# Delta rule: 16x16 diagonal blocks inverted by substitution on VectorE, chunks prepared ahead through DRAM

## The chip, the cores and the metric

One core of a Trainium2 chip runs the whole program in one launch. The metric is the device time in microseconds (us) of one execution. The kernel before was run three times: median 2832.96 us, from 2828.85 to 2835.94 us. One more execution was profiled.

## The reference, cut to what matters

The program is two transformer blocks over 1024 tokens of width 1024, in float32: a first mixer (retention beside a gated delta rule), a mixture of experts, a second mixer and an MLP. The change touches the gated delta rule alone. Per head and per chunk of tokens it computes

```python
a_mat = where(tri_strict, (k_beta @ k.T) * decay, 0.0)
t_mat = triangular_solve(eye + a_mat, eye, lower=True, unit_diagonal=True)
u = t_mat @ v_beta
w = t_mat @ (k_beta * exp(g))
attn = (q @ k.T) * decay
def step(state, inp):
    v_new = u_n - w_n @ state
    o_n = qg_n @ state + attn_n @ v_new
    state = state * gl_n + kt_n.T @ v_new
    return state, o_n
```

so one unit lower triangular matrix is inverted per head and chunk, and a state of 128x128 per head goes from chunk to chunk.

## The kernel before, in words

Every instruction is recorded first and placed later. The class `Program` takes each call with what it reads and writes (`record`, whose call of the engine is the line 346 that nearly all rows of the profile carry), gives it a price (`price`), and `flush` lists the instructions engine by engine with a list scheduler: an engine takes, of the instructions that are ready by the planned times, the one with the longest remaining path, and `prog.boost` is added to that length. The order is then fixed: on the chip every engine runs its own list in order and waits on semaphores. All loads and stores go through the one queue of SyncE (SP), also in a fixed order. Tiles are slots of two SBUF areas (`sbuf_61` for float32, `sbuf_62` for float32r in the listings of order below); a slot that is used again makes its new writer wait for the old readers. PSUM banks are handed out round robin by tag: `acc` has two, `dn` three, `tp`, `rs` and `rt` one each.

The first mixer (`mixer1`) makes the normed input, projects and convolves the delta rule's q, k and v into the DRAM buffer `qkv_d` (`dn_project`), and then records three things whose instructions the scheduler mixes:

- `dn_chunks` (line 1022), 8 chunks of 128 tokens with 4 heads, at boost 40000. Each 128x512 tile holds the four heads side by side.
- `tok_blocks`, boost 0: five blocks of 512 columns of `w_in` over 8 token tiles, each tile 24 float32r matmuls of 512 columns, evicted by ACT, DVE and POOL and stored to `rq_d`, `rk_d`, `rv_d`, `zg_d`; beside them eight half rows of `w_ada` are multiplied on DVE (`matvec`) and stored to `mod_d`.
- `retention`, 8 chunks, boost 40000; it needs what `tok_blocks` stores.

Then `mix_out` follows, the router, the experts, the second mixer and the MLP.

A chunk of `dn_chunks` loads k, q and v from `qkv_d`; transposes k, takes its norms, scales it (`kh`) and transposes it back (`khT`); makes the decays (`E`, `dN`, `dT`) and multiplies them with the products of `khT` with itself and with q. `dN` is then the strictly lower matrix to be inverted, `dT` the attention. The inverse is built by doubling in seven levels, b = 1, 2, 4, ... 64: `Uf` holds the inverse transposed and `Ti` the inverse, both right in blocks of b; a level masks the blocks that it adds out of `dN` (`AM`, on POOL) and runs

```python
mm(pp[:, h, :], AM[:, h, :], Uf[:, h, :], start=True, stop=True)
nc.scalar.activation(P, pp, AF.Copy)
mm(pu[:, h, :], Ti[:, h, :], P[:, h, :], start=True, stop=True)
nc.vector.tensor_tensor(out=Uf, in0=Uf, in1=pu, op=OP.subtract)
if b < 64:
    tr(pt[:, h, :], Uf[:, h, :], self.ident)
    nc.vector.tensor_copy(Ti, pt)
```

for h in 0 to 3, each step waiting for the one before on another engine. Level b = 1 needs only four transposes, two subtractions and a mask. After the levels come the products with the state `S`, the new state `Sn` and the output `o`, which is stored to `mix_d`.

Of the kernel before, what the change touches and what calls it, by code (L numbers as in the profile page):

```python
# [21 lines left out]
T = 1024  # L22
# [490 lines left out]
def shape_constants():  # L513
# [47 lines left out]
class Kern:  # L561
# [459 lines left out]

    def dn_chunks(self, A):
        nc, pd, sc = self.nc, self.pd, self.sc
        mm, tr = nc.tensor.matmul, nc.tensor.transpose
        S = None

        def bc(a, n=128):
            return a[:, :, None].to_broadcast([128, 4, n])

        lv = (1, 2, 4, 8, 16, 32, 64)  # L1030
        m3 = {b: A[f'm{b}'][:, None, :].to_broadcast([128, 4, 128]) for b in lv}
        eye3 = self.ident[:, None, :].to_broadcast([128, 4, 128])
        for n in range(NT):
            self.prog.boost = 40000.
            beta, G = sc['beta'][:, n], sc['G'][:, n]
            lq, lk, lv_ = [self.t(pd, [128, 4, 128], tag='ld' + c, bufs=2 if c == 'q' else 1) for c in 'qkv']
            for dst, i in ((lk, 1), (lq, 0), (lv_, 2)):
                nc.sync.dma_start(dst, self.qkv_d[:, 4 * i:4 * i + 4, n * 128:(n + 1) * 128])
            qT = lambda h: lq[:, h, :]

            ssk = self.t(pd, [128, 8], tag='ssk', bufs=2)
            junk = self.t(pd, [128, 128], tag='djunk', bufs=1)
            pk = self.ps([128, 4, 128], 'tp')
            for h in range(4):
                tr(pk[:, h, :], lk[:, h, :], self.ident)
            for h in range(4):
                nc.scalar.activation(junk, pk[:, h, :], AF.Square, accum_out=ssk[:, h:h + 1])
            rk = self.rstd(pd, ssk[:, 0:4], 4, 1.0, 'rk')
            kh = self.t(pd, [128, 4, 128], tag='kh', bufs=2)
            nc.vector.tensor_tensor(out=kh, in0=pk, in1=bc(rk), op=OP.mult)  # L1050
            pT = self.ps([128, 4, 128], 'tp')
            for h in range(4):
                tr(pT[:, h, :], kh[:, h, :], self.ident)
            khT = self.t(pd, [128, 4, 128], tag='khT', bufs=2)
            nc.scalar.activation(khT, pT, AF.Copy)
# [17 lines left out]
            nc.gpsimd.tensor_tensor(out=dT, in0=E, in1=A['negT'][:, None, :].to_broadcast([128, 4, 128]), op=OP.add)
            nc.scalar.activation(dT, dT, AF.Exp)
            pa = self.ps([128, 4, 128], 'dn')
            for h in range(4):
                mm(pa[:, h, :], khT[:, h, :], khT[:, h, :], start=True, stop=True)
            nc.vector.tensor_tensor(out=dN, in0=pa, in1=dN, op=OP.mult)
            pa = self.ps([128, 4, 128], 'dn')
            for h in range(4):  # L1080
                mm(pa[:, h, :], khT[:, h, :], qT(h), start=True, stop=True)
            nc.vector.tensor_tensor(out=dT, in0=pa, in1=dT, op=OP.mult)

            Uf = self.t(pd, [128, 4, 128], tag='U', bufs=2)
            Ti = self.t(pd, [128, 4, 128], tag='Ti', bufs=2)
            for b in lv:
                AM = self.t(pd, [128, 4, 128], tag='AM', bufs=2)
                (nc.vector if b == 1 else nc.gpsimd).tensor_tensor(out=AM, in0=dN, in1=m3[b], op=OP.mult)
                pp = self.ps([128, 4, 128], 'dn')
                if b == 1:  # L1090
                    for h in range(4):
                        tr(pp[:, h, :], AM[:, h, :], self.ident)
                    nc.vector.tensor_tensor(out=Uf, in0=eye3, in1=pp, op=OP.subtract)
                    nc.gpsimd.tensor_tensor(out=Ti, in0=eye3, in1=AM, op=OP.subtract)
                    continue
                for h in range(4):
                    mm(pp[:, h, :], AM[:, h, :], Uf[:, h, :], start=True, stop=True)
                P = self.t(pd, [128, 4, 128], tag='P', bufs=2)
                nc.scalar.activation(P, pp, AF.Copy)
                pu = self.ps([128, 4, 128], 'dn')  # L1100
                for h in range(4):
                    mm(pu[:, h, :], Ti[:, h, :], P[:, h, :], start=True, stop=True)
                nc.vector.tensor_tensor(out=Uf, in0=Uf, in1=pu, op=OP.subtract)
                if b < 64:
                    pt = self.ps([128, 4, 128], 'dn')
                    for h in range(4):
                        tr(pt[:, h, :], Uf[:, h, :], self.ident)
                    nc.vector.tensor_copy(Ti, pt)
            pv = self.ps([128, 4, 128], 'tp')
            for h in range(4):  # L1110
                tr(pv[:, h, :], lv_[:, h, :], self.ident)
            vb = self.t(pd, [128, 4, 128], tag='vb', bufs=1)
            nc.vector.tensor_tensor(out=vb, in0=pv, in1=bc(beta), op=OP.mult)

            if n:
                pw = self.ps([128, 4, 128], 'dn')
                for h in range(4):
# [4 lines left out]
            pv2 = self.ps([128, 4, 128], 'dn')
            for h in range(4):
                mm(pv2[:, h, :], Uf[:, h, :], vb[:, h, :], start=True, stop=True)
            vn = self.t(pd, [128, 4, 128], tag='vn', bufs=1)
            nc.scalar.activation(vn, pv2, AF.Copy)
            o = self.t(pd, [128, 4, 128], tag='o', bufs=1)
            if n:
                po = self.ps([128, 4, 128], 'dn')
                for h in range(4):  # L1130
                    mm(po[:, h, :], qT(h), S[:, h, :], start=True, stop=True)
                nc.vector.tensor_tensor(out=o, in0=po, in1=bc(sc['eG'][:, n]), op=OP.mult)
            po = self.ps([128, 4, 128], 'dn')
            for h in range(4):
                mm(po[:, h, :], dT[:, h, :], vn[:, h, :], start=True, stop=True)
            if n:
                nc.vector.tensor_tensor(out=o, in0=o, in1=po, op=OP.add)
            else:
                nc.vector.tensor_copy(o, po)
            if n < NT - 1:  # L1140
                ktl = self.t(pd, [128, 4, 128], tag='ktl', bufs=1)
                nc.gpsimd.tensor_tensor(out=ktl, in0=kh, in1=bc(sc['etail'][:, n]), op=OP.mult)
                pS = self.ps([128, 4, 128], 'dn')
                for h in range(4):
                    mm(pS[:, h, :], ktl[:, h, :], vn[:, h, :], start=True, stop=True)
                Sn = self.t(pd, [128, 4, 128], tag='S')
                if n:
                    for h in range(4):
                        nc.vector.scalar_tensor_tensor(Sn[:, h, :], S[:, h, :], sc['elast'][:, n, h:h + 1],
# [1137 lines left out]
```

## Time and profile before

| | us |
|---|---|
| median of 3 runs | 2832.96 |
| profiled execution, its own time | 2830.14 |
| span of the profile | 2828.1 |
| TensorE (PE) busy in the span | 2663.9 (94%) |
| delta rule, token blocks and retention side by side | about 213 to 660 |

The page gives the busy time of each engine, then the span in 40 slices with the busy share of a slice in tenths. A group of instructions is listed with its count, its busy time (overlaps counted once), the mean time of one, and the idle time of its engine just before it with what ended it. A matmul's time runs from its start to its modelled end, so successive ones overlap; the time that one occupies the engine is the busy time of a dense run through its count.

### The profile page before, as it was taken

The numbers are of one execution on the slowest core, as the hardware profiler recorded it, in microseconds if no ns is written. First come the engines' busy times: TensorE is split into PE (matmuls) and PEld (weight loads), VectorE is DVE, ScalarE is ACT, GpSimd is POOL, SyncE is SP. The second block draws the span as 40 slices with busy tenths as digits, with TensorE's granted clock in tenths as the row PEclk, the third lists the DMA queues.
The fourth block names the chain that finished last, engine by engine and source line by source line (L and its number), as shares of the span: only waits on it lengthen the run. The fifth ranks groups of instructions, "written<-read, shape, count | busy, mean of one in ns | idle before, by whom it ended". The sixth has DMA issues, their size and how long they took to land. (4 is left out here: it accounts for less than half of the span.)

```text
span 2828.1 us, 36441 instructions
## 1 busy us (share of the span) xinstructions
PE 2663.9 (94%) x13174; PEld 2048.9 (72%) x13174; DVE 1705.0 (60%) x2575; ACT 1117.4 (40%) x1960; POOL 622.5 (22%) x675
## 2 busy tenths in 40 slices
PE   5999999999978999999986999999999999999998
PEld 4787788997757776454435777777888888888886
DVE  7557676555679888786766335277445454444445
ACT  4333223333136677565545434357422212122122
POOL 2106433432442111322136012144110000000001
PEclk9999999999979999999998999999999999999999
DMA  9443246246348999999978343263211111111111
GB/s 243 91 138 88 93 149 165 80 157 230 143 165 287 344 349 341 352 323 361 341 245 295 121 125 110 72 172 94 94 42 52 38 52 52 45 52 53 45 53 67
DMA packets 305621, 446.82 MB, mean 158 GB/s; under 512 B 61274, under 2 KB 135694, under 8 KB 304414
## 3 DMA queue, kind: packets, MB, share of 16 engines
q1 hardware_dynamic: 298782, 427.68, 46.5%
q0 software_dynamic: 6656, 16.79, 1.7%
q8 instruction: 105, 1.72, 0.2%
q14 instruction: 78, 0.64, 0.1%
HBM read 384.54 MB, written 65.75 MB: 159 GB/s over the span
## 5 line engine op out<-in xcount | busy, mean ns | idle before, releaser
L346 PE MATMUL psum_all<-sbuf 128*128 128x512 f32 (+10 forms) x13174 | 2663.9, 363 | 151.7 <-DVE sbuf L346 99.9
L346 PEld LDWEIGHTS psum_all<-sbuf 128*128 128x128 f32 (+7 forms) x13174 | 2048.9, 176 | 766.3 <-issue 167.3
L346 ACT ACTIVATE sbuf<-sbuf 128x1024 fp32r<-128x1024 f32 (+9 forms) x792 | 707.6, 914 | 781.3 <-PE psum_all L346 536.3
L346 DVE TENSOR_TENSOR sbuf<-sbuf,sbuf 128x1024 fp32r<-128x1024 f32 (+3 forms) x538 | 616.8, 1166 | 277.6 <-ACT sbuf L346 269.0
L346 ACT ACTIVATE sbuf<-psum_all 128x512 f32<-128x512 f32 (+14 forms) x798 | 377.9, 485 | 886.1 <-PE psum_all L346 839.7
L346 POOL TENSOR_TENSOR sbuf<-sbuf 128x512 f32<-128x512 f32 (+7 forms) x325 | 384.3, 1190 | 576.7 <-DVE sbuf L346 474.4
L346 DVE TENSOR_TENSOR sbuf<-sbuf,psum_all 128x512 f32<-128x512 f32 (+4 forms) x359 | 239.1, 673 | 165.2 <-PE psum_all L346 164.6
L346 DVE TENSOR_TENSOR sbuf<-sbuf 128x512 f32<-128x512 f32 (+9 forms) x285 | 205.2, 734 | 203.6 <-ACT sbuf L346 175.5
L346 POOL TENSOR_SCALAR sbuf<-sbuf 128x1 f32<-128x1 f32 (+3 forms) x182 | 75.3, 415 | 994.9 <-ACT sbuf L346 902.7
L346 DVE TENSOR_TENSOR sbuf<-psum_all,sbuf 128x512 fp32r<-128x512 f32 (+13 forms) x306 | 182.3, 607 | 158.0 <-ACT sbuf L346 78.1
L346 DVE SCALAR_TENSOR_TENSOR sbuf<-sbuf 128x512 f32<-128x512 f32 (+5 forms) x247 | 196.3, 801 | 55.6 <-POOL sbuf L346 43.1
L346 DVE TENSOR_SCALAR sbuf<-sbuf 128x32 f32<-128x32 f32 (+7 forms) x220 | 111.2, 518 | 48.1 <-ACT sbuf L346 22.7
L1728 POOL DMA_INDIRECT y_d<-sbuf x35 | 57.4, 1641 | 195.8 <-DVE sbuf L346 194.5
L346 DVE SCALAR_TENSOR_TENSOR sbuf<-psum_all,sbuf 128x128 f32<-128x128 f32 (+9 forms) x109 | 62.0, 585 | 40.0 <-PE psum_all L346 39.5
L1716 POOL DMA_INDIRECT sbuf<-h_d,sbuf x35 | 45.1, 1288 | 186.2 <-PE psum_all L346 153.2
L346 DVE SCALAR_TENSOR_TENSOR sbuf<-sbuf,psum_all 128x128 f32<-128x128 f32 (+1 forms) x100 | 38.2, 409 | 76.7 <-PE psum_all L346 51.8
L346 DVE CUSTOM_DVE_ANT_0 sbuf<-psum_all,sbuf 128x512 f32<-128x512 f32 (+2 forms) x80 | 48.1, 613 | 24.8 <-PE psum_all L346 24.2
L346 DVE COPY sbuf<-psum_all 128x512 f32<-128x512 f32 (+9 forms) x55 | 31.7, 576 | 39.9 <-PE psum_all L346 39.7
L346 POOL MEMSET sbuf<- 64x64 f32 (+10 forms) x54 | 16.8, 313 | 174.4 <-DVE sbuf L346 91.9
L346 POOL TENSOR_TENSOR sbuf<-sbuf,sbuf 128x1024 fp32r<-128x1024 f32 x16 | 40.1, 2510 | 61.7 <-ACT sbuf L346 48.4
L346 ACT ACTIVATE sbuf<-psum_all,sbuf 128x128 f32<-128x128 f32 (+1 forms) x72 | 24.4, 405 | 23.4 <-PE psum_all L346 17.7
L346 ACT ACTIVATION_READ_ACCUMULATOR sbuf<-sbuf 128x1 f32 x152 | 28.9, 190 | 0.0
(18 smaller groups left out, 111.8 us busy)
## 6 DMA issues: line engine op xcount, KB each, us to landing
sbuf<-in_w SPq DMA_DIRECT2D x384, 512.0 KB
sbuf<-in_w_ff SPq DMA_DIRECT2D x64, 512.0 KB
sbuf<-in_w_in SPq DMA_DIRECT2D x56, 512.0 KB
sbuf<-in_w_ada SPq DMA_DIRECT2D x48, 512.0 KB
sbuf<-in_x SPq DMA_DIRECT2D x16, 512.0 KB
sbuf<-in_w_out SPq DMA_DIRECT2D x16, 512.0 KB
sbuf<-y_d SPq DMA_DIRECT2D x8, 1024.0 KB
qkv_d<-sbuf SPq DMA_DIRECT2D x12, 512.0 KB
```

Source lines behind the costliest of these rows:

```text
L346: op = self.new_op(eng, lambda: real(*a, **k), name, reads, writes)
L1716: return self.prog.real.gpsimd.indirect_dma_start(out=xg, out_offset=None, in_=self.h2_d, in_offset=bass.IndirectOffsetOnAxis(ap=tok, axis=0),
L1728: st = self.prog.real.gpsimd.indirect_dma_start(out=self.y_d, out_offset=bass.IndirectOffsetOnAxis(ap=dest, axis=0), in_=y, in_offset=None ...
```

## The change

The seven levels become three, b = 16, 32 and 64. What the first four made, the inverses of the 16x16 diagonal blocks, is made by forward substitution on VectorE instead. Four chunks of four heads have 128 such blocks, so each partition takes one, and 30 small instructions (15 steps of a product and a subtraction over 15 to 64 elements) serve four chunks. To bring a block into one partition, `dN` goes to the DRAM buffer `nb_d` and is read back as 128x16x16 in runs of 64 bytes; the inverses and their transposes go through `xb_d`, and each chunk reads its own as 128x4x32 in runs of 128 bytes and spreads them with the mask `blk` into `Uf` and `Ti`.

`dn_chunks` is cut in three: `dn_pre` (norms, transposes, decays, `dN`, `dT`), `dn_blocks` (the substitution) and `dn_scan` (the levels, the state, the output). As chunks are prepared well before their scans, `kh`, `khT`, `dN` and `dT` of a chunk (128x2048, 1 MB) are stored to `pre_d` and loaded again by the scan into a tile `prw` with one buffer; q is loaded twice.

```diff
-    for b in (1, 2, 4, 8, 16, 32, 64):
+    a.add('blk', i[:, None] // 16 == i[None, :] // 16)
+    for b in (16, 32, 64):
...
+        self.prog.boost = 40000.
+        for n in range(4):
+            self.dn_pre(A, n)
+        self.dn_blocks(0)
+        self.dn_scan(A, 0)
+        self.dn_pre(A, 4)
+        self.dn_pre(A, 5)
+        self.dn_scan(A, 1)
+        self.dn_pre(A, 6)
+        self.dn_pre(A, 7)
+        self.dn_blocks(1)
+        for n in range(2, 8):
+            self.dn_scan(A, n)
...
+        nc.vector.tensor_tensor(out=dN, in0=pa, in1=dN, op=OP.mult)
+
+        nc.sync.dma_start(self.dram_ap(self.nb_d, 4 * 16512 * n, [[128, 128], [16512, 4], [1, 128]]), dN)
...
+        nc.vector.tensor_tensor(out=dT, in0=pa, in1=dT, op=OP.mult)
+        nc.sync.dma_start(self.pre_d[n * 128:(n + 1) * 128], W.rearrange("p a h e -> p (a h e)"))
+
+    def dn_blocks(self, s):
+
+        nc, pd, V = self.nc, self.pd, self.nc.vector
+        N = self.t(pd, [128, 512], tag='P', bufs=2)[:, 0:256].rearrange("p (i j) -> p i j", j=16)
+        nc.sync.dma_start(N, self.dram_ap(self.nb_d, 128 * 2064 * s, [[2064, 128], [128, 16], [1, 16]]))
+        X = self.t(pd, [128, 16, 2, 16], tag='AM', bufs=2)
+        Y = self.t(pd, [128, 512], tag='P', bufs=2)[:, 0:256].rearrange("p (i j) -> p i j", j=16)
+        flat = X.rearrange("p i t j -> p (i t j)")
+        V.memset(flat, 0.0)
+        V.memset(flat[:, 0:512:33], 1.0)
+        for i in range(15):
+            r = [128, 15 - i, i + 1]
+            y, x = Y[:, i + 1:, 0:i + 1], X[:, i + 1:, 0, 0:i + 1]
+            V.tensor_tensor(out=y, in0=N[:, i + 1:, i:i + 1].to_broadcast(r),
+                            in1=X[:, i:i + 1, 0, 0:i + 1].to_broadcast(r), op=OP.mult)
+            V.tensor_tensor(out=x, in0=x, in1=y, op=OP.subtract)
+        V.tensor_copy(X[:, :, 1], X[:, :, 0].rearrange("p i j -> p j i"))
+        nc.sync.dma_start(self.xb_d[128 * s:128 * s + 128], flat)
+
+    def dn_scan(self, A, n):
...
+        lq, lv_ = [self.t(pd, [128, 4, 128], tag='ld' + c, bufs=1) for c in 'qv']
+        C = self.t(pd, [128, 4, 2, 16], tag='bC', bufs=2)
+        W = self.t(pd, [128, 4, 4, 128], tag='prw', bufs=1)
+        nc.sync.dma_start(W.rearrange("p a h e -> p (a h e)"), self.pre_d[n * 128:(n + 1) * 128])
+        nc.sync.dma_start(C.rearrange("p h t j -> p h (t j)"),
+                          self.dram_ap(self.xb_d, 32 * 512 * n, [[32, 128], [4096, 4], [1, 32]]))
...
+        for eng, t, x in ((nc.gpsimd, 1, Uf), (nc.vector, 0, Ti)):
+            eng.tensor_tensor(out=x.rearrange("p h (k j) -> p h k j", j=16), in1=blk,
+                              in0=C[:, :, t:t + 1, :].to_broadcast([128, 4, 8, 16]), op=OP.mult)
+        for b in (16, 32, 64):
...
```

The masks of levels 1 to 8 leave the constant `k_a`, whose load shrinks from 1864 to 1480 columns. The program before has 11765 matmuls and transposes, the changed one 11445.

The instructions of all engines differ up to the router's setup in `mix_out`; from there on they stand in the same order. Three places matter.

On TensorE, early in the first chunk before. A row of 128x128 from `sbuf_61` is a step of the delta rule (four heads), a row of 128x512 from `sbuf_62` is the token blocks:

```order
L346 MATMUL psum_all<-sbuf_61 128x128 x4
L346 MATMUL psum_all<-sbuf_62 128x512 x5
L346 MATMUL psum_all<-sbuf_61 128x128 x4
L346 MATMUL psum_all<-sbuf_62 128x512 x6
L346 MATMUL psum_all<-sbuf_61 128x128 x8
L346 MATMUL psum_all<-sbuf_62 128x512 x5
L346 MATMUL psum_all<-sbuf_61 128x128 x4
L346 MATMUL psum_all<-sbuf_62 128x512 x6
L346 MATMUL psum_all<-sbuf_61 128x128 x8
```

And now, where the four chunks are prepared and the first substitution runs:

```order
L346 MATMUL psum_all<-sbuf_61 128x128 x12
L346 MATMUL psum_all<-sbuf_62 128x512 x17
L346 MATMUL psum_all<-sbuf_61 128x128 x4
L346 MATMUL psum_all<-sbuf_62 128x512 x6
L346 MATMUL psum_all<-sbuf_61 128x128 x4
L346 MATMUL psum_all<-sbuf_62 128x512 x46
L346 MATMUL psum_all<-sbuf_61 1x512
L346 MATMUL psum_all<-sbuf_62 128x512 x59
L346 MATMUL psum_all<-sbuf_61 128x128 x4
L346 MATMUL psum_all<-sbuf_62 128x512 x5
L346 MATMUL psum_all<-sbuf_61 128x128 x4
L346 MATMUL psum_all<-sbuf_62 128x512 x6
```

The pattern of a level, 4, then 5, then 4, then 6, then 8, came straight after the preparation; now 46 and 59 matmuls of the token blocks stand between the preparation and the first level, and the second substitution has 30, 29 and 36 in the same way.

On VectorE, the first substitution (128x15 to 128x2x14 are its products and subtractions; 128x4x64 are the rotary products of the token blocks, 128x1024 a weight split):

```order
L346 TENSOR_TENSOR sbuf_61<-sbuf_61 128x15 x2
L346 TENSOR_TENSOR sbuf_61<-sbuf_61 128x4x64
L346 TENSOR_TENSOR sbuf_61<-sbuf_61 128x14x2 x2
L346 TENSOR_TENSOR sbuf_61<-sbuf_61 128x13x3 x2
L346 TENSOR_TENSOR sbuf_61<-sbuf_61 128x12x4 x2
L346 TENSOR_TENSOR sbuf_61<-sbuf_61 128x11x5 x2
L346 TENSOR_TENSOR sbuf_62<-sbuf_61,sbuf_62 128x1024
L346 TENSOR_TENSOR sbuf_61<-sbuf_61 128x10x6 x2
L346 TENSOR_TENSOR sbuf_61<-sbuf_61 128x9x7 x2
L346 TENSOR_TENSOR sbuf_61<-sbuf_61 128x8x8 x2
```

Where before a chunk's subtractions and copies from PSUM stood between the products of the token blocks, 30 small instructions stand now, once for four chunks; with the two shown, 11 instructions of the token blocks and of `matvec` stand among them: seven of 128x4x64, three of 128x512 and one of 128x1024.

On SP's queue, what a chunk asked for before, between the store of the chunk ahead and its own steps:

```order
L346 DMA mix_d<-sbuf_61 128x512
L346 DMA sbuf_61<-in_w_in 128x2x512 x2
L346 DMA sbuf_61<-in_w_ada 128x2x512
L346 DMA sbuf_61<-qkv_d 128x4x128 x2
L346 DMA sbuf_61<-in_w_ada 128x2x512 x2
```

and now, from the store of the first substitution to the load of the second scan's 1 MB:

```order
L346 DMA xb_d<-sbuf_61 128x512
L346 DMA sbuf_61<-in_w_ada 128x2x512
L346 DMA rk_d<-sbuf_61 128x512
L346 DMA sbuf_61<-in_w_ada 128x2x512
L346 DMA mod_d<-sbuf_61 1x512
L346 DMA sbuf_61<-xb_d 128x4x32 x2
L346 DMA sbuf_61<-in_w_ada 128x2x512
L346 DMA rk_d<-sbuf_61 128x512
L346 DMA sbuf_61<-in_b_ada 1x512
L346 DMA sbuf_61<-xb_d 128x4x32 x2
L346 DMA rk_d<-sbuf_61 128x512 x2
L346 DMA sbuf_61<-pre_d 128x2048
```

The store of the inverses and the loads that wait for it stand in line with the stores of the token blocks (`rk_d`) and the loads of `w_ada`.

## Rows read from the trace of the kernel before

**Rows 1.** The page, part 1: busy time of each engine in the span.
```profile
PE 2663.9 (94%) x13174; PEld 2048.9 (72%) x13174; DVE 1705.0 (60%) x2575; ACT 1117.4 (40%) x1960; POOL 622.5 (22%) x675
```
**Rows 2.** Stretches: busy us (x count) of each engine, PE clock, DMA share, GB/s.
```profile
213.00:300.00 87.00, 80.60 (x483) 67.60 (x482) 60.29 (x92) 30.77 (x92) 52.19 (x49) 0.98 0.35 97
900.00:1520.00 620.00, 572.72 (x2395) 339.90 (x2395) 481.21 (x518) 375.22 (x480) 148.94 (x106) 0.98 0.95 335
213.00:660.00 447.00, 429.50 (x2763) 372.52 (x2762) 276.59 (x461) 150.86 (x454) 189.25 (x190) 1.00 0.44 130
```
**Rows 3.** Groups by form, PE, 213 to 660 us.
```profile
L346 PE MATMUL psum_all<-sbuf 128*128 128x512 f32 x899 | 243.2, 407 | 0.0
L346 PE MATMUL psum_all<-sbuf 128*128 128x128 f32 x1844 | 232.3, 276 | 17.5 <-DVE sbuf L346 12.9 <-DMA sbuf<-rq_d 2.9 <-ACT sbuf L346 1.2
```
**Rows 4.** Groups by form, PE, 577.8 to 585.7 us: only float32 steps of 128 columns.
```profile
L346 PE MATMUL psum_all<-sbuf 128*128 128x128 f32 x73 | 8.3, 275 | 0.0
```
**Rows 5.** Groups by form, PE, 175 to 197 us: only float32r matmuls of 512 columns.
```profile
L346 PE MATMUL psum_all<-sbuf 128*128 128x512 f32 x99 | 22.6, 389 | 0.0
```
**Rows 6.** Timeline of DVE in one chunk: start us, us, instruction [idle before].
```profile
289.43 0.69 DVE L346 COPY sbuf<-psum_all 128x512 f32<-128x512 f32 x1
...
294.20 0.69 DVE L346 COPY sbuf<-psum_all 128x512 f32<-128x512 f32 x1 [1.81 <-PE psum_all L346]
```
**Rows 7.** Groups by form, DVE, 213 to 660 us.
```profile
L346 DVE TENSOR_TENSOR sbuf<-sbuf,psum_all 128x512 f32<-128x512 f32 x63 | 43.0, 682 | 37.3 <-PE psum_all L346 36.8
L346 DVE SCALAR_TENSOR_TENSOR sbuf<-sbuf 128x512 f32<-128x512 f32 x49 | 39.0, 796 | 2.1 <-DMA sbuf<-in_w_ada 1.6
L346 DVE TENSOR_TENSOR sbuf<-sbuf,sbuf 128x1024 fp32r<-128x1024 f32 x18 | 23.3, 1293 | 9.4 <-ACT sbuf L346 7.1 <-PE psum_all L346 2.1
L346 DVE TENSOR_TENSOR sbuf<-sbuf 128x256 f32<-128x256 f32 x64 | 38.3, 622 | 19.2 <-ACT sbuf L346 16.8 <-POOL sbuf L346 2.1
L346 DVE TENSOR_TENSOR sbuf<-sbuf 128x512 f32<-128x512 f32 x16 | 14.9, 929 | 0.3
L346 DVE SCALAR_TENSOR_TENSOR sbuf<-sbuf 128x4 f32<-128x4 f32 x16 | 9.6, 600 | 14.5 <-POOL sbuf L346 14.5
L346 DVE SCALAR_TENSOR_TENSOR sbuf<-sbuf 128x32 f32<-128x32 f32 x2 | 0.4, 185 | 0.0
```
**Rows 8.** Groups by form, POOL and ACT, 213 to 660 us.
```profile
L346 POOL TENSOR_TENSOR sbuf<-sbuf 128x512 f32<-128x512 f32 x93 | 121.8, 1320 | 180.3 <-DVE sbuf L346 128.1 <-PE psum_all L346 50.8 <-ACT sbuf L346 0.7
L346 POOL TENSOR_TENSOR sbuf<-sbuf 128x256 f32<-128x256 f32 x32 | 27.2, 856 | 45.0 <-DVE sbuf L346 44.8
L346 ACT ACTIVATE sbuf<-psum_all 128x512 f32<-128x512 f32 x103 | 60.6, 596 | 209.3 <-PE psum_all L346 209.3
```
**Rows 9.** Waits of SP's queue, 213 to 660 us: us in total, times, longest us.
```profile
SPq L346 <- DVE sbuf L346: 231.9, 86, 12.8
SPq L346 <- DMA mix_d<-sbuf: 10.9, 6, 3.5
SPq L346 <- DMA mod_d<-sbuf: 8.1, 4, 4.6
```
**Rows 10.** Waits of engines for loads out of DRAM buffers, whole span.
```profile
DVE sbuf L346 <- DMA sbuf<-y_d: 9.5, 1, 9.5
```
**Rows 11.** Waits of PE for loads out of DRAM buffers, 213 to 660 us.
```profile
PE psum_all L346 <- DMA sbuf<-rq_d: 2.9, 2, 2.0
```
**Rows 12.** DMA issues, whole span: count, KB each.
```profile
sbuf<-y_d SPq DMA_DIRECT2D x8, 1024.0 KB
```
**Rows 13.** Instructions on two buffers: ns min/median/max, first and last start us.
```profile
L346 SPq DMA_DIRECT2D sbuf<-qkv_d x24: 360/370/499, 169.3 to 548.5; - x24
...
L346 SPq DMA_DIRECT2D mod_d<-sbuf x8: 239/246/253, 267.7 to 480.5; - x8
L346 SPq DMA_DIRECT2D sbuf<-mod_d x6: 286/350/1002, 631.2 to 668.9; - x6
```

More of the change, by code (lines that the diff above doesn't have):

```diff
@@ L1031, in dn_chunks @@
[L1031 to L1043, printed above, removed]
+        beta, G = sc['beta'][:, n], sc['G'][:, n]
@@ new lines, in dn_pre @@
+        for h in range(4):
+            nc.scalar.activation(junk, pq[:, h, :], AF.Square, accum_out=ssk[:, 4 + h:5 + h])
+        self.rq8.append(self.rstd(pd, ssk[:, 4:8], 4, 1.0, f'rq{n}', bufs=1))
+        pg = self.ps([128, 4, 128], 'dn')
+        for h in range(4):
+            tr(pg[:, h, :], G[:, h:h + 1].to_broadcast([128, 128]), self.ident)
+        E = self.t(pd, [128, 4, 128], tag='E', bufs=1)
+        nc.vector.tensor_tensor(out=E, in0=pg, in1=bc(G), op=OP.subtract)
+        nc.gpsimd.tensor_tensor(out=dN, in0=E, in1=A['bigN'][:, None, :].to_broadcast([128, 4, 128]), op=OP.add)
@@ new lines, in dn_pre @@
+        nc.scalar.activation(dN, dN, AF.Exp, scale=-1.0)
+        nc.gpsimd.tensor_tensor(out=dN, in0=dN, in1=bc(beta), op=OP.mult)
+        nc.gpsimd.tensor_tensor(out=dT, in0=E, in1=A['negT'][:, None, :].to_broadcast([128, 4, 128]), op=OP.add)
+        nc.scalar.activation(dT, dT, AF.Exp)
+        pa = self.ps([128, 4, 128], 'dn')
+        for h in range(4):
+            mm(pa[:, h, :], khT[:, h, :], khT[:, h, :], start=True, stop=True)
+        nc.vector.tensor_tensor(out=dN, in0=pa, in1=dN, op=OP.mult)
@@ L1073, in dn_chunks @@
[L1073 to L1081, printed above, removed]
@@ L1122, in dn_chunks @@
[L1122 to L1132, printed above, removed]
+                nc.vector.scalar_tensor_tensor(vb[:, h, :], pw[:, h, :], sc['nbeG'][:, n, h:h + 1], vb[:, h, :],
+                                               op0=OP.mult, op1=OP.add)
@@ new lines, in dn_scan @@
+        po = self.ps([128, 4, 128], 'dn')
+        for h in range(4):
+            mm(po[:, h, :], dT[:, h, :], vn[:, h, :], start=True, stop=True)
+        if n:
+            nc.vector.tensor_tensor(out=o, in0=o, in1=po, op=OP.add)
+        else:
+            nc.vector.tensor_copy(o, po)
+        if n < NT - 1:
+            ktl = self.t(pd, [128, 4, 128], tag='ktl', bufs=1)
+            nc.gpsimd.tensor_tensor(out=ktl, in0=kh, in1=bc(sc['etail'][:, n]), op=OP.mult)
+            pS = self.ps([128, 4, 128], 'dn')
+            for h in range(4):
+                mm(pS[:, h, :], ktl[:, h, :], vn[:, h, :], start=True, stop=True)
+            Sn = self.t(pd, [128, 4, 128], tag='S')
@@ L1136, in dn_chunks @@
             if n:
-                nc.vector.tensor_tensor(out=o, in0=o, in1=po, op=OP.add)
-            else:
[L1139 to L1149, printed above, removed]
-                                                       pS[:, h, :], op0=OP.mult, op1=OP.add)
-                else:
-                    nc.vector.tensor_copy(Sn, pS)
-                S = Sn
```

173 lines of the change are left out of this document (96 added, 77 removed).

## The prediction

> **What bounds the kernel now.** I read the page first: PE is busy in 94% of the span, no other engine in more than 60% [rows 1]. Then the table of stretches, to see whether that average holds where the change works: from 213 to 660 us PE is busy 429.5 of 447.0 us at a granted clock of 1.00, so 17.5 us are idle, while DVE has 276.6 us, POOL 189.3, ACT 150.9, and the DMA engines are used to 0.44 [rows 2]. This stretch is bound by PE's work, not by the chain of chunks: the chain waits often, but the token blocks fill the waits. The timeline shows it in one chunk: a level of the doubling returns every 4.77 us (289.43 to 294.20) [rows 6], and order has 10 or 11 float32r matmuls in it. Groups by form split the stretch [rows 3]: 899 records of 512 columns, 1844 of 128. What one occupies is read from dense runs: 22.6 us for 99 records of 512 columns, 0.228 us each [rows 5]; 8.3 us for 73 records of 128 columns, of which some 0.16 us is the last one's tail, so 0.112 us each [rows 4]. A transpose is one such record; a float32 matmul of 128 columns is two (the program has 11765 matmuls and transposes, the trace 13174 records [rows 1]).
>
> **PE: the work that goes.** Per chunk, levels 2, 4 and 8 have 4 + 4 matmuls (16 records) and 4 transposes each, and level 1 has 4 transposes: 3 x 20 + 4 = 64 records, 512 for eight chunks. At 0.112 us this is **-57.3 us**, all on the bound engine. From below it is 512 x 0.108 = -55 us (73 records in the 7.9 us of that window); from above, by busy time through count in the whole stretch, 232.3 / 1844 = 0.126 us, -64.5 us [rows 3, 4]. I take 0.112, since it is the dense run's.
>
> **Waits that go.** PE waited 12.9 us for DVE before float32 steps [rows 3]; four of seven levels go, so at most 7 us of that, at least nothing, as the scheduler may pack the rest as tightly. I take **-3 us**.
>
> **The other engines.** DVE loses per chunk one mask (0.93 us), four subtractions and three copies (0.68 each), 5.7 us, or 45 us in all, and gains 7 us for `Ti` and two passes of the substitution of 15 to 30 us with what stands around it [rows 7]; POOL loses four products of 1.32 us and gains one per chunk, -32 us; ACT loses 24 evictions of 0.60 us, -14 us [rows 8]. None is the bound, so these count as nothing: what hides them is PE's own 370 us and more; without that cover they would be gains. SP issues 44 more transfers at about 0.37 us [rows 13], 16 us on a queue that sits in waits for over 230 us here [rows 9]. The transfers add about 22 MB (8 x 1 MB out and in, the rest small) to 130 GB/s x 447 us = 58 MB: 80 MB in about 390 us is 205 GB/s, and the experts' stretch shows 335 GB/s at a share of 0.95 [rows 2]. So the bandwidth costs nothing in the mean. The smaller `k_a` saves a load at the start that nothing of this stretch waits for: nothing.
>
> **New wait 1: the two substitution passes.** The first level of a scan now hangs on store `dN`, load, 30 DVE steps, store, load, then `Ti`, `Uf` and a mask. PE runs in order, so if this is late, the token blocks' matmuls behind the first level stand too; so do, on SP, the `rk_d` stores and `w_ada` loads behind the waiting transfers, and with the stores the evictions that want their buffers. The price is not in the trace, so by bounds. Four steps through DRAM: SP waited 8.1 us in 4 times for stores to `mod_d` to land and 10.9 in 6 for `mix_d`, so 1.8 to 4.6 us each (longest) [rows 9]; I take 2.0, 8 us, ends 7.2 and 18.4. Thirty small DVE steps: 0.185 us by 128x32, 0.600 us by 128x4 beside busy POOL [rows 7]; I take 0.30, nearer the first because most steps are of its size and follow no POOL result, 9 us, ends 5.6 and 18. The 11 instructions of others among them: 7 x 0.62 + 3 x 0.80 + 1.29 = 8 us [rows 7]. `Ti` and the mask: 0.93 + 1.32 = 2.2 us [rows 7, 8]. Sum 27.2 us, ends 23 and 46.6. The cover by order: 46 + 59 matmuls, 105 x 0.228 = 23.9 us, in the first pass, 30 + 29 + 36 = 95, 21.7 us, in the second. So 3.3 + 5.5 = **+9 us**, ends +1 and +48.
>
> POOL is busy 52.2 of 87 us when the first pass runs, with products of 0.86 to 1.32 us [rows 2, 8]. The Trainium skill, SBUF — State Buffer, section "Who interferes with whom", speaks against the change here: a DVE instruction with two SBUF inputs and a GpSimd instruction that reads SBUF exclude each other, and whichever issues second stands until the other ends; all 30 steps are such. By that rule a step that meets POOL (6 in 10) would wait about half a product, 0.33 us, 0.5 us a step, and the two passes would cost an estimated +22 us instead of +9. The 0.600 us rows agree with it in direction; no row shows it for a step of this kind.
>
> **New wait 2: the scans' reload.** `prw` has one buffer, so a scan's 1 MB load starts after the last reader of the scan before, and its masks wait for it: 7 times. The ends: PE lost 2.9 us in all to 24 loads of retention [rows 11], so nothing per load; or 9.5 us, which DVE once waited for a load of `y_d`, also of 1 MB [rows 10, 12]. I take 1 us each, **+7 us**, ends 0 and 66: the scheduler has put the token blocks' matmuls and retention into this wait, and the retention loads, which are placed in the same way, are the nearer rows.
>
> **Sum.** -57.3 - 3 + 9 + 7 = -44 us against the profiled execution's 2830.1 (span 2828.1 and 2 around it): 2786. The median of the runs is 2.8 above it, so **2788 us**. What follows keeps its order from the router on and moves along.
>
> **Rivals.** No change means within 0.3%, 8.5 us, about what a measurement of this kernel can tell.
> - *More is gained.* Both passes hide and the removed levels take their waits along: -64.5 - 7 to -60 gives 2761 to 2773. For it: DVE gets freer, and fewer handoffs are left. Against: the second cover, 21.7 us, is shorter than even the lowest sum of a pass, 23. Chance 0.14.
> - *The passes are exposed.* Each of the 30 steps at 0.600 us is 18 us, a pass 36.2, the two cost 12.3 + 14.5 = 27 us: -57.3 - 3 + 27 + 7 = -26, 2806. For it: POOL's 60% [rows 2]; against: before, nearly all such steps followed a POOL result. The mechanism is that of the page above. Chance 0.14.
> - *The reload becomes the bound, and the kernel slower.* Every scan waits for its 1 MB as DVE once did: 7 x 9.5 = 66 us, -57.3 - 3 + 9 + 66 = +15, 2848. It is slower than before from 7.4 us a scan ((57.3 + 3 - 9) / 7). For it: one buffer, and SP's queue in order; against: 0.44 use of the DMA engines [rows 2] and what retention's reloads cost [rows 11]. Chance 0.07.
> - *The change does not shorten the whole.* The stretch ends earlier, but `mix_out` waits for something that did not move, such as the rows of `mod_d`: 2833. Against: the last of them is stored at 480.5 us and first read at 631.2 [rows 13], 150 us of slack. Chance 0.05.
>
> **The numbers.** The forecast, -30 to -60 us (2773 to 2803), has 0.60. With the passes' rival up to 2818 and the upper part of the larger gain from 2768 this makes 8 in 10: 2768 to 2818. Faster by over 0.3%: 0.60 + 0.14 + 0.14 = 0.88; within: 0.05; slower: 0.07.
>
> **What would show it.** In the profile after, PE should have 512 records less and a stretch of about 400 us instead of 447 with 20 to 35 us of PE idle. Two gaps of 3 to 6 us before the first levels of scans 0 and 2 would confirm the passes' price; gaps over 12 us, with DVE's small steps at 0.6 us, the second rival. PE or POOL waiting for `pre_d` tells the reload's price: over 7 us a scan, and the forecast falls. If the stretch shortens and the next one grows by as much, the last rival holds.

## The result, and the profile after

The changed kernel takes 2789.51 us in the median of four runs (2786.89 to 2792.8), the kernel before 2831.74 beside it: a ratio of 0.985 (95% interval 0.9833 to 0.9868), 42.2 us less. The forecast was 2788, faster by 44. In the profiled execution (2788.22 us, span 2786.4) PE has exactly 512 records fewer than in [rows 1]. The page of the changed kernel, part 1:

```profile
PE 2612.6 (94%) x12662; PEld 1996.7 (72%) x12662; DVE 1676.1 (60%) x2585; ACT 1106.3 (40%) x1936; POOL 601.4 (22%) x651
```

Nearly all of the time leaves in the stage of the change. The table of stretches (busy us and count of PE, PEld, DVE, ACT, POOL, then clock, DMA share, GB/s), cut at the last `qkv_d` store, the last `mix_d` store and two later points that answer to each other (the stretch between the second and the third row, 140.5 us before and 138.6 after, is left out); first before:

```profile
209.40:656.10 446.70, 429.20 (x2762) 372.26 (x2761) 275.94 (x461) 153.81 (x459) 187.96 (x189) 1.00 0.44 130
656.10:709.70 53.60, 47.96 (x247) 37.05 (x245) 34.27 (x62) 16.19 (x27) 12.40 (x16) 1.00 0.61 208
850.20:2828.10 1977.90, 1899.56 (x8867) 1414.72 (x8865) 1163.17 (x1597) 831.17 (x1280) 325.79 (x347) 0.99 0.49 163
```

The same stretches after:

```profile
211.30:617.90 406.60, 381.03 (x2282) 323.18 (x2280) 250.89 (x473) 142.22 (x436) 165.20 (x167) 0.99 0.64 199
617.90:667.80 49.90, 41.78 (x209) 32.54 (x208) 32.00 (x60) 14.60 (x25) 9.78 (x14) 0.90 0.63 211
806.40:2786.40 1980.00, 1901.52 (x8867) 1415.69 (x8865) 1165.29 (x1597) 831.61 (x1280) 325.17 (x347) 0.99 0.49 163
```

The stretch fell from 446.7 to 406.6 us ("about 400" was forecast), with 25.6 us of PE idle (20 to 35 were forecast). The hand-over behind it is 3.7 us shorter but holds more idle: 8.1 us where there were 5.6. The long rest, 1980.0 against 1977.9 us, moved along.

So that runs whose routing differs can be compared too, one mark serves below: the start of the **eighth load of `mix_d`** on SP, by which all token blocks of the stage are done. It is read in one profiled execution of each kernel. The four executions of the changed kernel lie 5.9 us apart in the whole, so a difference of 2 or 3 us at the mark decides nothing. The instructions on that buffer, before and after (the last figure of "first and last start"):

```profile
L346 SPq DMA_DIRECT2D sbuf<-mix_d x8: 319/320/847, 645.3 to 778.2; - x8
```
```profile
L346 SPq DMA_DIRECT2D sbuf<-mix_d x8: 319/320/338, 604.5 to 736.4; - x8
```

The mark comes 41.8 us earlier, nearly the whole gain.

PE by form in the stage, 213 to 618 us; this answers to [rows 3]:

```profile
L346 PE MATMUL psum_all<-sbuf 128*128 128x512 f32 x921 | 240.5, 406 | 2.8 <-ACT sbuf L346 2.8
L346 PE MATMUL psum_all<-sbuf 128*128 128x128 f32 x1332 | 167.3, 277 | 22.7 <-DVE sbuf L346 6.6 <-POOL sbuf L346 5.0 <-DMA sbuf<-qkv_d 4.0
```

1844 records of 128 columns became 1332 and 232.3 us became 167.3. The wait for DVE in front of them was halved, 12.9 to 6.6 us, but waits for POOL and for a load came in. The waits for the buffers of the change, 213 to 620 us:

```profile
DVE sbuf L346 <- DMA sbuf<-nb_d: 10.7, 1, 10.7
POOL sbuf L346 <- DMA sbuf<-pre_d: 8.7, 5, 2.8
PE psum_all L346 <- POOL sbuf L346: 5.0, 5, 1.4
PE psum_all L346 <- DMA sbuf<-qkv_d: 4.0, 1, 4.0
```

POOL's masks wait for the reload five times, at most 2.8 us; DVE stands once for the diagonal blocks, 10.7 us. What happened there is told with the third and fourth runs.

### The profile page after: what moved, and what is told of

Read it like the earlier page. It is cut to its first block, busy times and chain, and to the rows that moved or that the text cites. A ratio compares the mean times of both kernels' runs of the same rounds, so it can differ in the third digit from the quotient of the medians.

```text
span 2786.4 us, 35368 instructions
## 1 busy us (share of the span) xinstructions
PE 2612.6 (94%) x12662; PEld 1996.7 (72%) x12662; DVE 1676.1 (60%) x2585; ACT 1106.3 (40%) x1936; POOL 601.4 (22%) x651
## 5 line engine op out<-in xcount | busy, mean ns | idle before, releaser
L346 PE MATMUL psum_all<-sbuf 128*128 128x512 f32 (+7 forms) x12662 | 2612.6, 367 | 161.3 <-DVE sbuf L346 94.7
L346 PEld LDWEIGHTS psum_all<-sbuf 128*128 128x128 f32 (+4 forms) x12662 | 1996.7, 176 | 776.8 <-issue 166.9
L346 ACT ACTIVATE sbuf<-psum_all 128x512 f32<-128x512 f32 (+14 forms) x774 | 364.6, 482 | 824.7 <-PE psum_all L346 769.9
L346 POOL TENSOR_TENSOR sbuf<-sbuf 128x512 f32<-128x512 f32 (+9 forms) x301 | 357.4, 1196 | 505.0 <-DVE sbuf L346 349.3
L346 DVE TENSOR_TENSOR sbuf<-sbuf 128x512 f32<-128x512 f32 (+16 forms) x345 | 212.2, 628 | 214.6 <-ACT sbuf L346 168.4
L346 DVE TENSOR_TENSOR sbuf<-sbuf,psum_all 128x512 f32<-128x512 f32 (+3 forms) x327 | 217.6, 673 | 157.0 <-PE psum_all L346 156.9
L346 POOL TENSOR_SCALAR sbuf<-sbuf 128x1 f32<-128x1 f32 (+3 forms) x182 | 81.9, 452 | 1034.3 <-ACT sbuf L346 938.2
L346 DVE TENSOR_TENSOR sbuf<-psum_all,sbuf 128x512 f32<-128x512 f32 (+12 forms) x306 | 182.5, 608 | 153.9 <-ACT sbuf L346 79.0
L346 DVE COPY sbuf<-psum_all 128x512 f32<-128x512 f32 (+9 forms) x31 | 15.2, 491 | 23.0 <-PE psum_all L346 23.0
```

The source lines that it names most:

```text
L346: op = self.new_op(eng, lambda: real(*a, **k), name, reads, writes)
```

## The experiments

Twelve kernels ran. Kernels that leave out part of the computation route tokens differently: they load expert weights (`in_w`) 396 to 468 times, where the kernels before and after load them 384 times. So their total says little, and they are read at the mark. (From the fifth run on, the letters of the theories are each run's own.)

| run | mark, us | median, us | ratio to before (interval) |
|---|---|---|---|
| before | 778.2 | 2831.7 | 1 |
| changed | 736.4 | 2789.5 | 0.985 (0.9833 to 0.9868) |
| 1 levels only | 717.4 | 2903.1 | routing differs |
| 2 staging, flawed | 896.1 | 2953.3 | 1.0423 |
| 3 wide load | 737.4 | 2830.0 | routing differs |
| 4 two steps | 736.1 | 3095.0 | routing differs |
| 5 no pass | 726.9 | 2913.2 | routing differs |
| 6 staging alone | 796.2 | 2847.6 | 1.0052 (1.0031 to 1.0072) |
| 7 split reload | 729.5 | 2782.7 | 0.9825 (0.9806 to 0.9845) |
| 8 quarters | 736.5 | 2788.5 | 0.9833 (0.9814 to 0.9852) |
| 9 pass not read | 728.8 | 2911.3 | routing differs |
| 10 and no load of C | 729.6 | 2909.1 | routing differs |
| 11 split and quarters | 735.7 | 2788.9 | 0.9844 (0.9823 to 0.9865) |
| 12 split, pass on GpSimd | 742.6 | 2794.4 | 0.9864 (0.9847 to 0.988) |

**1. The removed levels alone**, in the kernel before:

```diff
-        lv = (1, 2, 4, 8, 16, 32, 64)
+        lv = (16, 32, 64)
+            for eng, x in ((nc.gpsimd, Uf), (nc.vector, Ti)):
+                eng.tensor_tensor(out=x, in0=eye3, in1=eye3, op=OP.mult)
```

> The kernel before with levels 16, 32 and 64 alone; Uf and Ti start as the identity, so the inverses of the 16x16 blocks are left out of the computation. No substitution, no trip through DRAM, no preparation ahead. Theory A (the gain is PE's removed work): 512 records of 0.112 us less and some 3 us of waits: 2831.7 - 60 = 2772. Rival B (the chain of chunks, not PE's work, set the stretch, and most of the gain comes from preparing ahead): at most half of the gain without it, 2800 to 2815.

Measured: 717.4, 60.8 us below before. Stretches from 211 us to the mark, first of before, then of this run:

```profile
211.00:778.20 567.20, 538.73 (x3327) 456.34 (x3325) 356.44 (x658) 182.64 (x518) 228.54 (x246) 1.00 0.44 138
```
```profile
211.00:717.40 506.40, 481.75 (x2821) 403.29 (x2819) 313.37 (x600) 173.20 (x505) 203.44 (x222) 0.99 0.51 155
```

PE's busy time fell by 57.0 us and its idle time from 28.5 to 24.7, 3.8: the first two terms of the sum, -57.3 and -3, at their sizes. The changed kernel, 19.0 us later, therefore pays 19 for staging and passes, where 16 were forecast. Its own row to the mark shows in what coin:

```profile
211.00:736.40 525.40, 486.33 (x2818) 404.39 (x2816) 329.25 (x667) 171.32 (x496) 203.29 (x222) 0.98 0.60 192
```

PE is idle for 39.1 us, 14.4 more than in the first run, and busy for 4.6 more with three records less, at a clock of 0.98 against 0.99. So some 14 of the 19 us are waits and some 5 are slower matmuls, for which the forecast had no term.

**2. Staging alone, first attempt.** All seven levels, chunks prepared ahead, nothing through `nb_d`; the room was found by letting retention use the delta rule's scratch tile (`tag='rjunk'` became `tag='djunk'`).

> The changed kernel with all seven levels on PE and without the substitution and its buffers: preparation ahead and the 1 MB trip through DRAM alone. Theory A: PE's records as before, the reload's waits on top: 2831.7 + 7 = 2839, between 2829 and 2845. Rival B: preparing ahead is what gains: 2790 to 2815.

Measured: 2953.3 us. That edit chained retention to the delta chunks, and it ran behind them; the stretches of this run at 600 to 800 us show PE starving and its clock falling with it:

```profile
600.00:700.00 100.00, 62.05 (x354) 53.43 (x352) 38.20 (x62) 25.29 (x65) 23.71 (x24) 0.80 0.49 162
700.00:800.00 100.00, 55.88 (x256) 47.80 (x257) 17.07 (x40) 17.12 (x57) 6.74 (x12) 0.62 0.20 69
```

The last load of retention's `rq_d` comes at 774.9 us here and at 641.6 before, and PE waits 52.8 us in all for the eight loads of that buffer, against 2.9. The time lies outside both theories. The run tells nothing of the staging, but it shows what it costs when the token blocks' work no longer covers the chunks.

**3. The load of diagonal blocks in 128 runs of 1 KB** instead of 2048 of 64 B (the values are then others than the diagonal blocks):

```diff
-[[2064, 128], [128, 16], [1, 16]]
+[[2064, 128], [1, 256]]
```

> The changed kernel; the substitution's load of 128x16x16 in runs of 64 bytes is replaced by one of 128x256 in runs of 1 KB from the same buffer, so the numbers of the blocks are not those asked for. Theory C (the cost of the passes is SP's queue, which stood 5.5 us behind each load of 2048 short runs, with loads behind it that PE wanted): 2789.5 - 5 to - 8, 2782 to 2785. Rival D (the cost is the latency of the pass, as forecast): the load lands a few us earlier, 1 to 3 us gained, 2787 to 2789.

**4. Two of the 15 steps of a pass** (the inverse of the diagonal blocks is then incomplete): `range(15)` became `(0, 14)`.

> The changed kernel with 2 of the 15 substitution steps (4 of the 30 small instructions); the rest of the inversion is left out. Theory C: the steps are covered, so within 2 us of 2789.5. Rival D (the latency of the pass is exposed): 26 steps of 0.2 to 0.3 us less in each pass, up to the 9 us that the passes were forecast to cost: 2781 to 2784.

Measured: 737.4 and 736.1, within 1 us of the changed kernel. The third run misses both of its theories, which had the mark earlier; in the fourth, theory C holds. A pass that is cheaper by most of its steps, or whose load has a sixteenth of the runs, gains nothing at the mark. The timeline of SP in the changed kernel shows why the load's shape does not matter (start us, us, instruction):

```profile
395.23 0.37 SPq L346 DMA_DIRECT2D nb_d<-sbuf  x1
395.82 0.36 SPq L346 DMA_DIRECT2D pre_d<-sbuf  x1
396.96 0.37 SPq L346 DMA_DIRECT2D sbuf<-in_w_in  x1
397.38 0.84 SPq L346 DMA_DIRECT2D sbuf<-qkv_d  x1
401.50 0.36 SPq L346 DMA_DIRECT2D sbuf<-nb_d  x1
401.95 5.50 SPq L346 DMA_DIRECT2D rv_d<-sbuf  x1
```

The 1 MB store of `pre_d` and a 512 KB weight load go out just ahead of the blocks' load. The stretches on both sides of that load's issue, up to the first step at 408.60:

```profile
395.00:401.50 6.50, 6.36 (x31) 5.02 (x30) 2.62 (x4) 1.96 (x10) 1.45 (x2) 1.00 1.05 284
401.50:408.60 7.10, 3.09 (x14) 2.35 (x14) 0.00 (x0) 0.00 (x0) 0.00 (x0) 0.90 1.01 247
```

The DMA engines are full all the time, and for 7.1 us DVE, ACT and POOL start nothing. In the third run the same step took 7.3 us (403.91 to 411.20), in the eighth, with a quarter of the runs left to load, 7.0 (402.75 to 409.77). Three shapes, one time, at a DMA share of 1.01 to 1.07.

Is it the store of `pre_d` that fills the engines? In the eleventh run, below, it goes out 2 us behind the last quarter of the blocks' load:

```profile
397.68 0.34 SPq L346 DMA_DIRECT2D sbuf<-nb_d  x1
399.69 1.01 SPq L346 DMA_DIRECT2D pre_d<-sbuf  x1
```

The first step still came 7.0 us behind that load (404.70), again at a share of 1.01. In the seventh run the load in its first shape goes out behind the store and takes 3.5 us to the first step, at a share of 0.63:

```profile
401.70:405.20 3.50, 3.50 (x17) 2.92 (x16) 0.00 (x1) 2.49 (x3) 0.00 (x0) 1.00 0.63 129
```

So the shape does not set this time, and it goes with how full the DMA engines are: 7.0 to 8.6 us at shares from 0.93 (the ninth run) to 1.07, and 4.7 and 3.5 at 0.62 and 0.63 (the twelfth and the seventh). That the one store is what fills them is not shown. Nor does the mark pay for this stand: in the third and eighth runs PE was busy all through it.

**5. No pass at all** (the diagonal blocks are left uninverted):

```diff
-        self.dn_blocks(0)
-        self.dn_blocks(1)
...
-        nc.sync.dma_start(self.dram_ap(self.nb_d, 4 * 16512 * n, [[128, 128], [16512, 4], [1, 128]]), dN)
```

> The changed kernel without the substitution: no nb_d store, no pass, no xb_d store, no load of C; Uf and Ti start as the identity, so the diagonal blocks are left uninverted; dn_pre, pre_d, the reload of prw and levels 16, 32, 64 stay. The routing and with it the experts' time may shift, so the stage is read at the start of the eighth load of mix_d on SP: 778.2 us in the kernel before, 736.4 in the changed one, 717.4 in the kernel before with levels 16 to 64 only. So 19.0 us are paid for staging and passes together. Theory A (as forecast: passes 9, reload 7): 724 to 728. Theory B (the reload is the whole cost, the passes are covered): 733 to 737. Theory C (the passes are the whole cost): 716 to 720.

Measured: 726.9. Staging costs 9.5 us over the first run, the passes 9.5 more: theory A of this run, beside 7 and 9 in the sum. But the last `mix_d` store does not come earlier without passes; first the changed kernel, then this run (the last start is the figure to read):

```profile
L346 SPq DMA_DIRECT2D mix_d<-sbuf x16: 319/320/1409, 343.1 to 617.9; - x16
```
```profile
L346 SPq DMA_DIRECT2D mix_d<-sbuf x16: 319/320/1272, 300.5 to 618.9; - x16
```

All of the passes' 9.5 us show up behind that store.

**6. Staging alone, second attempt**, with retention's tile its own.

> Staging without substitution, again: the chunks are prepared ahead through pre_d as in the changed kernel, but all seven levels run on PE and nothing goes through nb_d or xb_d. This time retention keeps its own scratch tile; the room comes from the scratch tile of the delta rule, whose squares go into dT before it is written and into Uf after its last use. Theory A (the reload costs 7 us, all else equal): 2835 to 2843 in all, against 2832 of the kernel before. Theory B (the reload costs up to 19): 2845 to 2853. Theory C (the staging gains by itself, since the preparation is off the chain of a chunk): 2815 to 2830.

Measured: 2847.6 us, 13.9 more than before beside it, and 18.0 at the mark: within theory B's range. But this edit has a price of its own. The waits of this run, 211 to 690 us:

```profile
ACT sbuf L346 <- DMA pre_d<-sbuf: 13.7, 5, 5.8
POOL sbuf L346 <- DMA sbuf<-pre_d: 10.4, 5, 4.2
```

ACT waits 13.7 us for the store of `pre_d`, because the squares were put into the tile that it reads. So the 13.9 us hold more than the staging, and what staging costs in the changed kernel can't be read from them. That staging does not gain by itself is shown.

**7. The reload in pieces**, `dN` first and in a tile of its own:

```diff
+        D = self.t(pd, [128, 4, 128], tag='prn', bufs=1)
+        W = self.t(pd, [128, 3, 4, 128], tag='prw', bufs=1)
+        nc.sync.dma_start(D.rearrange("p h e -> p (h e)"), row[:, 1024:1536])
```

> The changed kernel with the reload in three loads and two tiles: dN alone into a tile prn, which the last level's mask releases early in a chunk, then kh and khT, then dT into prw. Theory A (the wait of the first mask for the reload is worth 7 us): 2781 to 2786 against 2789.5. Theory B (the reload is hidden by token-block matmuls): 2788 to 2792, no difference. Theory C (SP's queue is what is short, two more issues a chunk): 2791 to 2796.

Measured: 2782.7 us, 729.5 at the mark, 6.9 earlier: theory A by the time. It is the fastest kernel of the study, 51.0 us below the kernel before beside it (2833.73). Against the changed kernel the intervals of the ratios still overlap, and one of its five executions took 2790.95, so these 6.8 us are likely, not certain. The reason is not seen in the waits: POOL stands longer for the reload than in the changed kernel, where it was 8.7 us:

```profile
POOL sbuf L346 <- DMA sbuf<-pre_d: 14.8, 6, 6.7
```

**8. The blocks loaded in quarters**, each behind its own chunk's store (`[[2064, 128], ...` became four loads of `[[2064, 32], ...`).

> The changed kernel with the load of the diagonal blocks in four pieces of 32 partitions, each issued behind its own chunk's nb_d store, so that of 2048 runs of 64 B only 512 stand between the last chunk's store and the first step of a pass. Theory A (the passes' chains are exposed at their ends, 3.3 and 5.5 us): 2784 to 2787 against 2789.5. Theory B (the passes are covered and what is paid lies elsewhere): 2788 to 2792. Theory C (more short-run issues on SP delay the other loads): 2791 to 2797.

Measured: 2788.5, mark 736.5: theory B, as after the third run.

**9 and 10. The pass runs, but nothing reads it**: `Uf` and `Ti` start as the identity; in the tenth, `C` is not loaded either.

> The changed kernel with both passes, their stores and the loads of C in place, but Uf and Ti start as the identity instead of being masked out of C: the result of the substitution is left out, and no scan waits for it. Read at the start of the eighth load of mix_d: 736.4 us in the changed kernel, 726.9 without the passes (9.5 us less). Theory A (the 9.5 us are the wait of scans 0 and 2 for a pass and its two DRAM steps): 726 to 729. Theory B (they are the passes' own work and transfers, which stand in the way of others): 734 to 737. In between: both.

> As the run before, and without the eight loads of C, so that SP issues nothing that waits for the end of a pass; the substitution's result is left out here too. Theory A: as the run before, 726 to 729. Theory B1 (loads of C hold up the loads behind them on SP): 5 to 9 us below the run before. Theory B2 (the passes' work on VectorE and the buffers that they hold): within 2 us of the run before.

Measured: 728.8 and 729.6. The ninth run is in theory A, the tenth just outside it and within 1 us of the ninth, so the loads of `C` cost nothing that shows here. 7.6 of the 9.5 us go when the pass's result is not read; whether the other 2 are its own work can't be told at the mark. One wait for a pass stays all the same. POOL waits for a tile that the second pass holds until its store to `xb_d` is out; the changed kernel, then the ninth run:

```profile
POOL sbuf L346 <- DMA xb_d<-sbuf: 35.1, 1, 35.1
```
```profile
POOL sbuf L346 <- DMA xb_d<-sbuf: 32.8, 2, 32.5
```

And the last `mix_d` store moves by only 1.7 us (616.2 against 617.9). The other part is in the hand-over, where the token blocks have run out; PE's waits there, in the changed kernel from 617 to 668 us, then in the ninth run from 616 to 660:

```profile
PE psum_all L346 <- DVE sbuf L346: 7.8, 4, 4.4
```
```profile
PE psum_all L346 <- DVE sbuf L346: 4.0, 3, 2.0
```

**11. Both edits**, the split reload and the quarters.

> The two edits of the seventh and eighth runs together: dN reloaded by itself, and the diagonal blocks loaded in four pieces. Theory A (the pieces are worth nothing, the early dN stays worth 6.9 us of the stage): 2780 to 2786. Theory B (with the reload out of the way the passes' chains come to the front, and the pieces now count): 2774 to 2780. Theory C (two more kinds of issues on SP get in each other's way): 2787 to 2795.

Measured: 2788.9, mark 735.7. The 6.9 us of the split are gone again but for 0.7 us: the time is in the range of theory C. The intervals of the seventh and this run overlap. One place is visible: here VectorE makes 29 steps in one row (7.0 us from 404.70), and the roundings behind them come late. The waits of this run from 404 to 414 us:

```profile
ACT sbuf L346 <- DVE sbuf L346: 4.6, 1, 4.6
PE psum_all L346 <- ACT sbuf L346: 4.3, 1, 4.3
```

**12. The split reload with the pass on GpSimd** (`V` is `nc.gpsimd`).

> The seventh run (dN reloaded by itself, 2782.7 us, eighth load of mix_d at 729.5) with the whole substitution pass on GpSimd instead of VectorE. In the changed kernel VectorE stands 10.7 us for the second load of diagonal blocks and then makes 30 steps one behind the other; GpSimd there waits for the pass to give its tile back. Its 128x256 operations take 0.88 us and its 128x32 ones 0.25, so that a pass takes about 15 us instead of 7 to 9. Theory A (VectorE's standing holds up the evictions and roundings that PE waits for): 2775 to 2780. Theory B (a pass's place and length do not matter within such bounds, as 13 steps less did not): 2781 to 2786. Theory C (the longer pass is exposed in front of scans 0 and 2, twice 4 to 8 us): 2788 to 2800.

Measured: 2794.4, mark 742.6, 13.1 behind the seventh run: theory C by the time, but not by its reason. From the issue of the blocks' load to the pass's store it is 29.2 us in the first pass (266.8 to 296.0) and 20.8 in the second (407.4 to 428.2), in the seventh run 23.8 and 24.2: one longer, one shorter. What the stage shows instead is GpSimd late for others. Waits for POOL from 211 to 660 us, first in the seventh run, then here:

```profile
ACT sbuf L346 <- POOL sbuf L346: 24.1, 10, 5.0
PE psum_all L346 <- POOL sbuf L346: 1.7, 2, 1.3
```
```profile
ACT sbuf L346 <- POOL sbuf L346: 31.1, 10, 6.9
PE psum_all L346 <- POOL sbuf L346: 4.0, 1, 4.0
```

Groups by form of POOL in this run, same window:

```profile
L346 POOL TENSOR_TENSOR sbuf<-sbuf 128x48 f32<-128x48 f32 x8 | 3.9, 486 | 0.6
L346 POOL TENSOR_TENSOR sbuf<-sbuf 128x28 f32<-128x28 f32 x8 | 2.8, 350 | 0.6
```

In the mean, which may hold waits for VectorE, a step is about twice as long here as on VectorE, and behind the steps on GpSimd's queue stand products that ACT and PE need. Their added waits, 7.0 and 2.3 us, are most of the 13.1 in size; that they are its cause is argued, not shown.

## Why the prediction was right

**PE's work.** -57.3 from 0.112 us a record; 57.0 measured in the first run. The dense run [rows 4] was the right row; busy time through count, 0.126, would have given 64.5.

**Waits that go.** -3; 3.8 measured as idle time in the first run.

**New wait 1, the passes.** +9; 9.5 measured (first part of run 5), so the size was met. Its make-up was not. A step took not 0.30 us but 0.2, and the steps through DRAM not 2.0 but up to 7. Groups by form of DVE in the changed kernel, from 264 to 296 us and, in the second fence, from 408 to 433:

```profile
L346 DVE TENSOR_TENSOR sbuf<-sbuf 128x15 f32<-128x15 f32 x4 | 1.8, 451 | 0.0
L346 DVE TENSOR_TENSOR sbuf<-sbuf 128x63 f32<-128x63 f32 x4 | 0.9, 226 | 0.1
```
```profile
L346 DVE TENSOR_TENSOR sbuf<-sbuf 128x63 f32<-128x63 f32 x4 | 0.9, 221 | 0.1
L346 DVE TENSOR_TENSOR sbuf<-sbuf 128x15 f32<-128x15 f32 x4 | 0.7, 177 | 10.7 <-DMA sbuf<-nb_d 10.7
```

Over all forms of these two views the 30 steps sum to 8.2 us in the first pass and 6.1 in the second, not 9. The place was wrong as well: the two gaps of 3 to 6 us, which the prediction named as the sign of this price, did not appear. PE's timeline, 270 to 306 us (idle before in brackets), has 1.4 us twice near the first level of scan 0, and its largest gap ahead of them, while the steps are made:

```profile
278.40 19.40 PE L346 MATMUL psum_all<-sbuf 128*128 128x512 f32 x81 [2.84 <-ACT sbuf L346]
299.20 4.59 PE L346 MATMUL psum_all<-sbuf 128*128 128x128 f32 x27 [1.41 <-POOL sbuf L346]
305.14 1.04 PE L346 MATMUL psum_all<-sbuf 128*128 128x128 f32 x7 [1.35 <-DVE sbuf L346]
```

A gap like it stands in the fifth run, which has no pass, so it is no sign of the passes' price:

```profile
277.30 28.41 PE L346 MATMUL psum_all<-sbuf 128*128 128x128 f32 x152 [3.29 <-ACT sbuf L346]
```

Near the first level of scan 2 the gaps are 1.4 us at most, and the 4.0 us for `qkv_d` (in the waits above) fall around the second pass and are absent in the fifth run. The prediction also lets scan 2 hang on the data of the second pass. By the code each pass inverts the blocks of four chunks, so scans 2 and 3 read what the first pass wrote; what scan 2 waits for is the tile of the second pass, in the 35.1 us of POOL above. "The bandwidth costs nothing in the mean" is a sentence that misled: the mean share is 0.64, but around a pass it is 1.0. That 9 met 9.5 is luck as far as these runs show: the price came, but not by the chain that it was added up from.

**New wait 2, the reload.** +7; 9.5 measured for all of the staging, and 6.9 came back when `dN` was loaded by itself, but not in the eleventh run, which loads it so too. Within the bounds 0 to 66 and near the size taken. That it is the wait for the reload is not shown: POOL waits 8.7 us for it in all and PE 5.0 for POOL, and in the seventh run POOL waited more while the mark came earlier.

**Sum.** -57.3 - 3 + 9 + 7 = -44; measured -60.8 + 9.5 + 9.5 = -41.8 at the mark and -42.2 in the medians. The large terms, PE's work and its waits, are right by their mechanism. The two added waits are right in size, with a working that the runs do not bear out, and about 5 of their 19 us are slower matmuls: that part is luck.

**The rivals.** More gained (2761 to 2773) falls: both passes are paid. Steps at 0.6 us fall as a rule for all of them, but not as a mechanism: in the first pass four steps of 30 met a POOL product and took 0.65 to 0.74 us, and one such group shows it from 287.2 to 288.7 us:

```profile
L346 DVE TENSOR_TENSOR sbuf<-sbuf 128x15 f32<-128x15 f32 x2 | 1.4, 720 | 0.0
```

Alone the same step takes 0.177. The rule of the Trainium skill, SBUF — State Buffer, section "Who interferes with whom", agrees with these rows. What failed was the chance of meeting POOL: taken from POOL's busy share, 6 in 10, and found as 4 in 30 in the first pass; in the second no form of step is above 0.222 us in the mean. POOL stood waiting for DVE during much of the first pass, 9.2 us before 282.93 and 1.7 before 286.32. The reload as the bound falls: its longest wait is 2.8 us, far from the 7.3 that the prediction's 51.3 us make over seven scans (it has 7.4). That the whole does not shorten falls with the stretches above.

**What stays open.** Why steps saved (run 4) return nothing while a wait removed (run 9) returns 7.6; part of the answer is the hand-over, whose idle time moves by some 4 us between kernels that do not touch it. In run 4 the last `mix_d` store comes 7.0 us earlier (610.9) and in run 7 22.8 earlier (595.1), but their marks only 0.3 and 6.9: what leaves the stage is in part paid back behind it. Every edit also lets the scheduler place the token blocks anew, so differences of 5 to 7 us between variants, the seventh and eleventh runs among them, are not settled as to cause. Two buffers for `prw`, or tiles of their own for a pass, were not tried, so what the tiles that a pass holds cost is not separated from its data.

## What to carry to other kernels

Where PE bounds a stretch, price removed matmuls by a dense run of their form, and price what replaces them as waits with a cover that has an end; here the sum came out within 3 us, though the second price is not borne out in its parts. So check a price where it was predicted to be paid, and not only by its size. Look at the DMA share around the new transfer, not at its mean: a 128 KB load took 7 us to its first reader at a share of 1.0, whether it went in long runs, in short ones or had a quarter left to go, and 3.5 us at 0.63. And do not take an engine's busy share for the chance of meeting it when it waits for the very engine in question.

## What the runs showed of the hardware

- The issue behind a load of 2048 runs of 64 B took 4.67 and 5.50 us on SP in the changed kernel, and 3.23 to 7.27 in runs 4, 9, 10 and 12; in the second pass of run 7 the next issue came 2.2 us later and took 0.34. Behind 128 runs of 1 KB it took 1.16 and 0.38 (run 3), behind 512 runs of 64 B 1.04 (run 8). It holds up SP's queue, but the marks of runs 3 and 8 did not move by it.
- From that load's issue to its first reader it took 7.0 to 8.6 us at a DMA share of 0.93 to 1.07, and 3.5 and 4.7 at 0.63 and 0.62.
- GpSimd's small products took 0.35 to 0.49 us at 28 to 63 elements a partition in the mean (run 12, waits for VectorE possibly among them), VectorE's uncontended 0.18 to 0.22 for the same forms.
- A VectorE product with both inputs in SBUF went from 0.18 to 0.72 us beside a GpSimd product.
